# Weight splits of the even layer: three buffers for the high and low parts, two for the raw units, splits three units ahead

## The chip, the cores and the metric

The kernel runs on one core of a Trainium2 chip. The metric is the device time of one execution in microseconds (us). A difference of 0.2%, 2.4 us here, is about what its measurement can tell from no change. The core has five engines with in-order instruction queues: PE (TensorE, the matrix multiplies), DVE (VectorE), ACT (ScalarE), POOL (GpSimd) and SP (SyncE), which here issues nearly all transfers.

## The reference, cut to what matters

Two residual layers on `x` of 512 positions by 1024 channels, each followed by a squared-ReLU MLP; all in float32.

```python
def even_mixer(h, w_in, ..., w_out):
    proj = h @ w_in                       # u, q, k, v
    u = proj[..., :S5_WIDTH]
    q, k, v = jnp.split(proj[..., S5_WIDTH:], 3, axis=-1)
    q = rotary(rmsnorm(heads(q), q_g))
    k = rotary(rmsnorm(heads(k), k_g))
    y_a = s5_mixer(u, ...)                # state-space scan, gelu, gate
    y_b = dilated_attention(q, k, heads(v))
    return jnp.concatenate([y_a, y_b], axis=-1) @ w_out

for layer in range(2):
    h = rmsnorm(x, norm_mix_g[layer])
    x = x + (even_mixer(h, ...) if layer == 0 else mlstm_mixer(h, ...))
    h = rmsnorm(x, norm_mlp_g[layer])
    x = x + jnp.square(jax.nn.relu(h @ w1)) @ w2
```

## The kernel before, in words

**Weights.** Every weight matrix comes in units of 128x1024 floats. A unit is loaded into a raw buffer `wr` (L147), ACT copies it to a rounded high part `wh` (L160), and DVE subtracts to get the low part `wl` (L161). A product is then three multiplies: high by high, high by low, low by high (`mm3`, L172), so one unit of a projection is 24 multiplies of 128x512. `w_init` gets the list of units in the order in which they are used. `w_next` (L165) hands out the next unit, and `w_pump` (L151), called before and after, issues transfers and splits for the units that follow. In the even layer (`wp2` is None) there are three raw buffers and two pairs of `wh` and `wl`; transfers are issued three units ahead and splits made two ahead. From the first MLP on, `wp2` adds a third pair, and both distances grow by one.

**The even layer.** `EVEN_SEQ` (L30) writes out the order of its steps by hand: `u0` to `u3` project the state-space inputs; `a0` to `a3` and `b0` to `b3` the two halves of q and k; `v0` to `v3` the values; `n` and `r` normalise and rotate q and k; `C`, `K`, `E`, `T`, `B`, `O` and `G` are the state-space steps for one of four groups of channels Q; `h0` to `h34` are the attention steps; `X`, `Y` and the output projection close it. Counted from 0 in the order of use, the weight units are u0 a0 b0 u1 a2 u2 v0 v1 u3 v2 v3 b2 a1 a3 b1 b3, then two units of the gate and eight of the output projection. A scheduler takes the steps in that order, lets instructions that would wait be overtaken, and fixes the order of each engine's queue when the program is built. On the chip a queue stays in that order.

**Steps that the prediction speaks of.** `s5_params` (L488) computes the state-space coefficients; part of it runs on POOL (`gt`, L543) and ends in `s_pis`, `s_la` and `s_lb`. `s5_rot` (step `E`, L600) builds a table of rotations in `x` tiles by doubling: per step DVE multiplies with `s_pr`, multiplies with `s_pis` into a temporary `w0`, adds, and ACT copies halves across (L619, L620); then ACT makes `E` from it. `powers` (L628) makes `Z` and `CG`, with its temporary `w1`. `s5_in` (step `B`, L689) multiplies with `E`, scans (L710), multiplies again and gets `W`; ACT copies halves of `psa` and `W` across into `x` tiles (L705, L713). `s5_out` (step `O`, L724) sends its result through DRAM (tiles `du`), and `s5_gelu` (L741) takes it from there. `qk_rot` (L807) makes `rA` and `rB` from a transposed factor and sends them to the q and k tiles. `att_init` (L860) takes over the buffer `hg` of the activations when the last projection has read it, and loads the mask into it (`in_amask`). `att_scores` (L870) multiplies q and k on PE, adds the mask on DVE with a running maximum (L881, result `nm`), and takes the exponential on ACT (L885, after a table load).

Of the kernel before, what the change touches and what calls it, by code (L numbers as in the profile page):

```python
# [9 lines left out]
F32 = mybir.dt.float32  # L10
F32R = mybir.dt.float32r
# [5 lines left out]
P = 128  # L17
# [44 lines left out]
class Trunk:  # L62
# [67 lines left out]
            self.nc.sync.dma_start(out=self.dbg[name], in_=ap)  # L130


    AHEAD_DMA = 3
    AHEAD_SPLIT = 2
    RAW_BUFS = 3
    MORE_DMA = 1

    def w_init(self, units):
        self.wp2 = None
# [2 lines left out]

    def w_dma(self, n):
        while self.wd < n:
            r = self.t(self.wp, (P, 1024), "wr", F32, self.RAW_BUFS)
            u = self.units[self.wd]
            self.dma(r, u() if callable(u) else u)  # L147
            self.raw[self.wd] = r
            self.wd += 1

    def w_pump(self):  # L151
        n = 0 if self.wp2 is None else 1
        self.w_dma(min(self.wi + self.AHEAD_DMA + n * self.MORE_DMA, len(self.units)))
        while self.wsx < min(self.wi + self.AHEAD_SPLIT + n, len(self.units)):
            r = self.raw.pop(self.wsx)
            third = self.wp2 is not None and self.wsx % 3 == 2
            pool, bufs = (self.wp2, 1) if third else (self.wp, 2)
            h = self.t(pool, (P, 1024), "wh", F32R, bufs)
            l = self.t(pool, (P, 1024), "wl", F32R, bufs)
            self.copy_act(h, r)  # L160
            self.sub(l, r, h.bitcast(F32))  # L161
            self.split[self.wsx] = (h, l)
            self.wsx += 1
# [436 lines left out]
    def s5_rot(self, pool, Q):  # L600
        nc = self.nc
        gs = slice(8 * Q, 8 * Q + 8)
        v3 = lambda t: t.rearrange("p (g k) -> p g k", k=64)
        A, S = v3(self.xt(6)), v3(self.xt(7))
        nc.vector.memset(A[0:64, :, 0:1], 1.0)
        nc.vector.memset(A[64:128, :, 0:1], 0.0)
        nc.vector.memset(S[0:64, :, 0:1], 0.0)
        nc.vector.memset(S[64:128, :, 0:1], 1.0)
        self.copy_act(A[:, :, 1], self.e1[:, 0, gs])
        self.copy_act(S[:, :, 1], self.e1[:, 1, gs])  # L610
        for m in range(1, 6):
            n = 1 << m
            b = lambda x: x[:, m - 1, gs].unsqueeze(2).to_broadcast([P, 8, n])
            w = self.t(pool, (P, 8, n), "w0")
            self.mul(A[:, :, n:2 * n], A[:, :, 0:n], b(self.pr))
            self.mul(w, S[:, :, 0:n], b(self.pis))
            self.add(A[:, :, n:2 * n], A[:, :, n:2 * n], w)
            if m < 5:
                self.copy_act(S[0:64, :, n:2 * n], A[64:128, :, n:2 * n])  # L619
                self.copy_act(S[64:128, :, n:2 * n], A[0:64, :, n:2 * n])  # L620
        E = self.t(pool, (P, 2, 8, 64), "E", bufs=2)
        self.copy_act(E[0:64, 0], A[0:64])
        self.copy_act(E[64:128, 0], A[0:64])
        self.act(E[0:64, 1], A[64:128], AF.Copy, scale=-1.0)
        self.copy_act(E[64:128, 1], A[64:128])
        self.s5e[Q] = E
# [772 lines left out]
```

## Time and profile before

| | us |
|---|---|
| median of 3 runs | 1186.29 (1185.99 to 1187.22) |
| the profiled execution, whole | 1185.93 |
| its span, first to last instruction | 1184.1 |
| PE busy in it | 1161.5 (98%) |
| DVE busy | 813.4 (69%) |
| ACT busy | 643.1 (54%) |
| POOL busy | 64.1 (5%) |

Times inside the trace run from the start of the span. The even layer's projections stand in the first 134 us, its attention from there to about 208 us, its output projection to about 222 us; MLP, odd layer and second MLP follow. "Idle before" an instruction is the time in which its engine stood still, with the instruction that ended it. The granted clock is that of TensorE, 1.00 for 2.4 GHz and 0.50 for 1.2 GHz; a stretch in between is a mixture of the two.

### The profile page before, as it was taken

To read this page: it belongs to the slowest core of one execution; us is meant where nothing else is said; L and a number is where in the kernel's file an instruction comes from. 1 tells how busy PE (TensorE), PEld (TensorE's weight loads), DVE (VectorE), ACT (ScalarE), POOL (GpSimd) and SP (SyncE) were. 2 spreads that over 40 slices of the span, in tenths; PEclk is the share of its full clock that TensorE was granted. 3 is DMA by queue.
4 is the path that set the end of the run, shared out by engine and by line. 5 is a ranking of instruction groups with operands and counts; after the bars stand their busy time and mean duration, and the time that the engine had idled before them with its cause. 6 is when DMAs were issued, how large, how long until landed. Compare 5 with 4: busy or idle time off the path is not lost.

```text
span 1184.1 us, 15701 instructions
## 1 busy us (share of the span) xinstructions
PE 1161.5 (98%) x5540; PEld 956.2 (81%) x5540; DVE 813.4 (69%) x1466; ACT 643.1 (54%) x1162; POOL 64.1 (5%) x121
## 2 busy tenths in 40 slices
PE   6989999999999999999999999999999999999998
PEld 5868776788888888888888888887888888888887
DVE  8799864666457447779858975865664574477796
ACT  5467777444434446666656645544444444456664
POOL 0522220000000000000100000000000000000000
PEclk9989999999999999999999999999999999999999
DMA  6434531359999335565624333222599994346654
GB/s 236 125 95 122 143 79 58 121 202 370 351 345 357 122 120 160 194 195 172 188 90 153 107 108 107 81 89 72 182 353 367 345 350 144 111 157 195 208 185 158
DMA packets 73869, 216.56 MB, mean 183 GB/s; under 512 B 16888, under 2 KB 17992, under 8 KB 73792
## 3 DMA queue, kind: packets, MB, share of 16 engines
q1 hardware_dynamic: 72576, 214.27, 53.7%
q0 software_dynamic: 1216, 1.31, 0.5%
q8 instruction: 43, 0.70, 0.2%
q14 instruction: 34, 0.28, 0.1%
HBM read 175.14 MB, written 38.31 MB: 180 GB/s over the span
## 4 chain that ended last, share of the span: by engine, by line
PE 92%; DVE 3%; ACT 1%; POOL 1%; issue 1%; DMA 1%; SPq 0%; DVEq 0%; ACTq 0%
PE acc L123 79%; PE psa L123 8%; PE psb L123 3%; DVE wl L96 1%; PE psb L898 1%; POOL rA L543 1%; PE psb L281 1%; ACT wh L120 0%; ACT hg L117 0%; DVE hg L108 0%; DMA hg<-in_amask 0%; DMA wr<-in_w_l 0%; DVE x L108 0%; PE psb L1207 0%; DVE x L96 0%
## 5 line engine op out<-in xcount | busy, mean ns | idle before, releaser
L123 PE MATMUL acc<-hg,wh 128*128 128x512 f32 x1600 | 500.7, 393 | 8.8 <-ACT hg L117 7.2
L120 ACT ACTIVATE wh<-wr 128x1024 fp32r<-128x1024 f32 x243 | 257.2, 1060 | 398.1 <-PE acc L123 321.3
L96 DVE TENSOR_TENSOR wl<-wr,wh 128x1024 fp32r<-128x1024 f32 x243 | 297.3, 1224 | 221.5 <-ACT wh L120 211.4
L123 PEld LDWEIGHTS acc<-hg,wh 128*128 128x128 f32 x1600 | 298.7, 188 | 70.1 <-ACT hg L117 7.2
L123 PE MATMUL acc<-hg,wl 128*128 128x512 f32 x800 | 313.6, 392 | 0.6 <-DVE wl L96 0.6
L123 PE MATMUL acc<-wh,sp 128*128 128x512 f32 x768 | 223.0, 389 | 0.0
L123 PEld LDWEIGHTS acc<-hg,wl 128*128 128x128 f32 x800 | 150.7, 188 | 31.9 <-DVE wl L96 1.1
L123 PEld LDWEIGHTS acc<-wh,sp 128*128 128x128 f32 x768 | 144.2, 188 | 30.0
L123 PE MATMUL acc<-wl,sp 128*128 128x512 f32 x384 | 135.9, 390 | 0.8 <-DVE wl L96 0.8
L120 ACT ACTIVATE sp<-s 128x256 fp32r<-128x256 f32 x224 | 89.8, 409 | 6.8 <-PE acc L123 5.7
L96 DVE TENSOR_TENSOR tq<-tq,tq 128x1024 f32<-128x1024 f32 x64 | 78.2, 1222 | 21.0 <-DMA tq<-in_w2s 20.0
L96 DVE TENSOR_TENSOR sp<-s,sp 128x256 fp32r<-128x256 f32 x224 | 86.8, 417 | 1.4 <-ACT sp L120 1.4
L123 PEld LDWEIGHTS acc<-wl,sp 128*128 128x128 f32 x384 | 71.9, 188 | 16.6 <-DVE wl L96 1.6
L123 PE MATMUL acc<-wh,hg 128*128 128x512 f32 x192 | 63.0, 402 | 5.4 <-ACT wh L120 5.4
L123 PEld LDWEIGHTS acc<-wh,hg 128*128 128x128 f32 x192 | 36.6, 193 | 13.2 <-ACT wh L120 5.8
L123 PE MATMUL psa<-wh,sp 128*128 128x512 f32 x128 | 42.0, 389 | 0.0
L117 ACT ACTIVATE rr<-acc 128x512 f32<-128x512 f32 x72 | 41.6, 578 | 0.0
L117 ACT ACTIVATE s<-rr 128x512 f32<-128x512 f32 x64 | 40.4, 631 | 1.0
L123 PE MATMUL acc<-wl,hg 128*128 128x512 f32 x96 | 38.5, 401 | 0.3 <-DVE wl L96 0.3
L108 DVE SCALAR_TENSOR_TENSOR sf<-zb,cvw,sf 128x512 f32<-128x512 f32 x48 | 35.3, 747 | 2.3 <-ACT sf L117 1.8
L96 DVE TENSOR_TENSOR x<-x,acc 128x512 f32<-128x512 f32 x16 | 10.8, 686 | 29.3 <-PE acc L123 29.2
L123 PE MATMUL acc<-y,wh 128*128 128x512 f32 x96 | 30.0, 394 | 0.0
(324 smaller groups left out, 1327.7 us busy)
## 6 DMA issues: line engine op xcount, KB each, us to landing
wr<-in_w_l SPq DMA_DIRECT2D x67, 512.0 KB, 3.5
wr<-in_w SPq DMA_DIRECT2D x64, 512.0 KB, 5.2
tq<-in_w2s SPq DMA_DIRECT2D x64, 512.0 KB, 6.3
T<-tq SPq DMA_DIRECT2D x64, 512.0 KB, 4.8
wr<-T SPq DMA_DIRECT2D x64, 512.0 KB, 3.3
wr<-in_w2s SPq DMA_DIRECT2D x48, 512.0 KB, 4.0
x<-in_xT SPq DMA_DIRECT2D x16, 256.0 KB, 4.1
na<-scr SPq DMA_DIRECT2D x8, 256.0 KB, 3.7
```

Of the source, the lines that this page charges most:

```text
L96: return self.nc.vector.tensor_tensor(out=o, in0=x, in1=y, op=op)
L108: return self.nc.vector.scalar_tensor_tensor(out=o, in0=x, scalar=s, in1=y, op0=op0, op1=op1)
L117: return self.nc.scalar.activation(o, x, f, bias=bias, scale=scale, **kw)
L120: return self.nc.scalar.activation(o, x, AF.Copy)
L123: return self.nc.tensor.matmul(o, l, r, start=start, stop=stop)
L281: self.nc.tensor.transpose(p[:, k * P:(k + 1) * P], self.x[4 * n + k][:, t * P:(t + 1) * P], self.ident)
L543: gt = lambda o, x, y, op: self.nc.gpsimd.tensor_tensor(out=o, in0=x, in1=y, op=op)
L898: self.nc.tensor.transpose(t[:, k * P:(k + 1) * P], p[:, k * P:(k + 1) * P], self.ident)
```

## The change

In the even layer there are now three pairs of `wh` and `wl` and two raw buffers. Splits are made three units ahead and transfers issued four ahead. From the first MLP on the third raw buffer comes from `wp2`, and transfers go five ahead; there are three pairs and three raw buffers there as before. The temporary `w0` of `s5_rot` no longer has a tile of its own: it uses the tile `x2`, which `s5_in` uses too.

```diff
-    AHEAD_DMA = 3
-    AHEAD_SPLIT = 2
-    RAW_BUFS = 3
-    MORE_DMA = 1
+    AHEAD_DMA = 4
+    AHEAD_SPLIT = 3
...
     def w_dma(self, n):
         while self.wd < n:
-            r = self.t(self.wp, (P, 1024), "wr", F32, self.RAW_BUFS)
+            second = self.wp2 is not None and self.wd % 3 == 2
+            r = self.t(self.wp2 if second else self.wp, (P, 1024), "wr", F32, 1 if second else 2)
...
     def w_pump(self):
         n = 0 if self.wp2 is None else 1
-        self.w_dma(min(self.wi + self.AHEAD_DMA + n * self.MORE_DMA, len(self.units)))
-        while self.wsx < min(self.wi + self.AHEAD_SPLIT + n, len(self.units)):
+        self.w_dma(min(self.wi + self.AHEAD_DMA + n, len(self.units)))
+        while self.wsx < min(self.wi + self.AHEAD_SPLIT, len(self.units)):
             r = self.raw.pop(self.wsx)
-            third = self.wp2 is not None and self.wsx % 3 == 2
-            pool, bufs = (self.wp2, 1) if third else (self.wp, 2)
-            h = self.t(pool, (P, 1024), "wh", F32R, bufs)
-            l = self.t(pool, (P, 1024), "wl", F32R, bufs)
+            h = self.t(self.wp, (P, 1024), "wh", F32R, 3)
+            l = self.t(self.wp, (P, 1024), "wl", F32R, 3)
...
-            w = self.t(pool, (P, 8, n), "w0")
+            w = self.xt(2)[:, 0:8 * n].rearrange("p (g k) -> p g k", k=n)
```

The number of instructions on each engine stays as it was. What changes is the order in the queues: on PE, DVE and ACT in the even layer alone, on SP in the MLPs too. In the rows below the last number of a name counts tiles in the order in which the program made them, so it differs between the two kernels.

The first place is DVE's queue around the subtraction for unit 9 (v2), `wl_811` before and `wl_787` now. `x_86` before and `x_89` now is the table of step `E0`; `CG` belongs to step `K`; `wl_781` is the subtraction for unit 8. Before:

```order
L96 TENSOR_TENSOR wl_781<-wr_697,wh_780 128x1024
L96 TENSOR_TENSOR w_134_741<-x_133_734,s_pis_273 128x16
L96 TENSOR_TENSOR w_83_476<-bin_414,s_lb_317 128x8x48
L605 MEMSET x_132_733 64x8
L606 MEMSET x_132_733 64x8
L96 TENSOR_TENSOR CG_474<-CG_474,w_83_476 128x8x48
L96 TENSOR_TENSOR x_132_733<-x_132_733,s_pr_272 128x8x2
L96 TENSOR_TENSOR w_84_480<-bin_414,s_lb_317 128x8x48
L96 TENSOR_TENSOR x_132_733<-x_132_733,w_134_741 128x8x2
L96 TENSOR_TENSOR CG_474<-CG_474,w_84_480 128x8x48
L96 TENSOR_TENSOR x_132_733<-x_132_733,s_pr_272 128x8x4
L96 TENSOR_TENSOR wl_811<-wr_778,wh_810 128x1024
```

Now:

```order
L96 TENSOR_TENSOR x_94_520<-x_90_495,s_pis_273 128x128
L96 TENSOR_TENSOR x_89_494<-x_89_494,x_94_520 128x8x16
L96 TENSOR_TENSOR x_89_494<-x_89_494,s_pr_272 128x8x32
L96 TENSOR_TENSOR wl_787<-wr_703,wh_786 128x1024
L96 TENSOR_TENSOR x_95_526<-x_90_495,s_pis_273 128x256
L96 TENSOR_TENSOR x_89_494<-x_89_494,x_95_526 128x8x32
L604 MEMSET x_136_740 64x8
L605 MEMSET x_136_740 64x8
L96 TENSOR_TENSOR CG_480<-bin_420,s_la_316 128x8x48 x3
L96 TENSOR_TENSOR CG_845<-bin_677,s_la_316 128x8x48 x2
L96 TENSOR_TENSOR x_137_747<-x_136_740,s_pis_273 128x16
```

The subtraction for unit 9 has moved from behind most of step `K` to the middle of step `E0`. The one for unit 8 stands still earlier, ahead of the instruction that writes `s_pis`, as the one for unit 7 does. Ahead of POOL's part of `s5_params`, whose first instruction waits for a DVE instruction on `sf`, stand the subtraction for unit 6 and the two `x<-acc,r` of u0 and u1, which before stood behind it.

The second place is DVE's queue at the first mask sum of the attention (`nm_1550` before, `nm_1556` now). Before:

```order
L96 TENSOR_TENSOR CG_1495<-CG_1495,w_296_1505 128x8x48
L96 TENSOR_TENSOR wi_1453<-wi_1453,x_283_1454 128x512
L96 TENSOR_TENSOR wl_1513<-wr_1408,wh_1512 128x1024
L710 SCALAR_TENSOR_TENSOR W_1460<-ss_1441,wi_1453 128x512
L108 SCALAR_TENSOR_TENSOR qkv_1563<-vc_385,psb_1554 128x16
L108 SCALAR_TENSOR_TENSOR qkv_1587<-vc_385,psb_1578 128x16
L881 ISA hg_1543,nm_1550<-psa_1547,hg_1543 128x128
L881 ISA nm_1550 128x1
L96 TENSOR_TENSOR wi_1462<-W_1460,E_1368 128x512
```

Now:

```order
L96 TENSOR_TENSOR CG_1501<-CG_1501,w_299_1511 128x8x48
L96 TENSOR_TENSOR y_346_1708<-x_294_1498,y_346_1708 128x512
L96 TENSOR_TENSOR wi_1459<-wi_1459,x_286_1460 128x512
L108 SCALAR_TENSOR_TENSOR qkv_1569<-vc_391,psb_1560 128x16
L707 SCALAR_TENSOR_TENSOR W_1466<-ss_1447,wi_1459 128x512
L96 TENSOR_TENSOR wi_1468<-W_1466,E_1374 128x512
L96 TENSOR_TENSOR x_289_1469<-x_289_1469,E_1374 128x512
L717 MEMSET W_1474 128x8
L108 SCALAR_TENSOR_TENSOR qkv_1593<-vc_391,psb_1584 128x16
L878 ISA hg_1549,nm_1556<-psa_1553,hg_1549 128x128
L878 ISA nm_1556 128x1
```

Everything that stood ahead of the first mask sum still does. New ahead of it are `wi_1468` and `x_289` of step `B3`, the low part `y` of the gelu of step `G1`, and further up the subtraction for unit 18 (the first of the output projection). The instructions of step `E3`, which stood apart with those of steps `r0` and `r2` between them, now follow one another without a break, behind the subtraction for unit 17.

## Rows read from the trace of the kernel before

**Rows 1.** The page: busy us and share of the span of each engine.
```profile
PE 1161.5 (98%) x5540; PEld 956.2 (81%) x5540; DVE 813.4 (69%) x1466; ACT 643.1 (54%) x1162; POOL 64.1 (5%) x121
```
**Rows 2.** PE's waits: who waited for whom, us in total, times, longest.
```profile
PE acc L123 <- ACT wh L120: 5.8, 3, 5.4
```
**Rows 3.** Busy by stretch: start:end, us, PE PEld DVE ACT POOL, PEclk, DMA.
```profile
67.90:134.00 66.10, 66.09 (x404) 57.28 (x405) 64.19 (x149) 46.51 (x90) 12.03 (x17) 0.98 0.45 129
134.00:146.00 12.00, 11.54 (x75) 7.83 (x74) 9.69 (x27) 11.81 (x26) 6.13 (x2) 0.86 0.44 131
146.00:208.00 62.00, 60.58 (x357) 42.94 (x357) 35.76 (x93) 46.34 (x109) 8.66 (x16) 1.00 0.25 68
222.00:1185.00 963.00, 956.29 (x4415) 794.84 (x4413) 638.33 (x1004) 495.34 (x849) 14.72 (x36) 1.00 0.58 197
```
**Rows 4.** PE in order of time: start us, us, instruction [idle before <-releaser].
```profile
65.57 2.07 PE L123 MATMUL acc<-wh,hg 128*128 128x512 f32 x4 [5.39 <-ACT wh L120]
67.91 0.79 PE L123 MATMUL acc<-wl,hg 128*128 128x512 f32 x1 [0.27 <-DVE wl L96]
137.56 4.38 PE L123 MATMUL psa<-k,hg 128*128 128x128 f32 x8
```
**Rows 5.** Busy by stretch, behind PE's long wait.
```profile
65.57:70.20 4.63, 4.36 (x9) 2.97 (x10) 4.63 (x14) 1.03 (x5) 0.00 (x0) 0.50 0.55 176
70.20:75.00 4.80, 4.80 (x38) 3.70 (x36) 3.99 (x13) 2.04 (x6) 0.00 (x0) 0.99 0.10 42
```
**Rows 6.** ACT in order of time, around the long wait of PE.
```profile
61.27 1.27 ACT L120 ACTIVATE E<-x 64x512 f32<-64x512 f32 x2 [1.16 <-DVE x L96]
64.47 1.04 ACT L120 ACTIVATE wh<-wr 128x1024 fp32r<-128x1024 f32 x1
```
**Rows 7.** Busy by stretch, before the attention.
```profile
17.60:62.00 44.40, 42.54 (x206) 35.48 (x206) 37.50 (x130) 18.86 (x51) 19.42 (x42) 1.00 0.41 119
62.00:138.20 76.20, 72.36 (x444) 62.46 (x444) 74.00 (x168) 54.49 (x105) 13.24 (x20) 0.96 0.45 130
```
**Rows 8.** The chain that ended last, at the attention's start: start us, us, what.
```profile
134.26 3.82 DMA hg<-in_amask
138.23 0.29 DVE hg L881
...
139.83 1.28 ACT L117
```
**Rows 9.** DVE in order of time.
```profile
46.58 1.11 DVE L96 TENSOR_TENSOR x<-acc,r 128x512 f32<-128x512 f32 x1 [2.69 <-PE acc L123]
48.51 0.30 DVE L112 TENSOR_SCALAR s_pis<-s_pis,cst 128x160 f32<-128x160 f32 x1 [0.81 <-POOL s_pis L543]
...
125.53 1.19 DVE L96 TENSOR_TENSOR wl<-wr,wh 128x1024 fp32r<-128x1024 f32 x1
126.65 0.68 DVE L96 TENSOR_TENSOR rA<-ev,sf 128x512 f32<-128x512 f32 x1
127.25 0.68 DVE L96 TENSOR_TENSOR rB<-ev,sf 128x512 f32<-128x512 f32 x1
```
**Rows 10.** POOL in order of time, in its part of `s5_params`.
```profile
38.15 0.43 POOL L543 TENSOR_TENSOR rA<-rA 128x32 f32<-128x32 f32 x2 [35.53 <-DVE sf L96]
...
42.89 1.10 POOL L543 TENSOR_TENSOR s_pis<-rA 128x32 f32<-128x32 f32 x1
...
45.25 0.24 POOL L543 TENSOR_TENSOR s_pis<-rA 128x32 f32<-128x32 f32 x1
```
**Rows 11.** ACT in order of time, copies across of steps `E` and `B`, then the first exponential.
```profile
106.29 0.47 ACT L120 ACTIVATE x<-x 64x32 f32<-64x32 f32 x2 [0.90 <-DVE x L96]
...
138.54 1.27 ACT L120 ACTIVATE x<-W 64x512 f32<-64x512 f32 x2
...
141.12 0.40 ACT L117 ACTIVATE hg<-hg,nm 128x128 f32<-128x128 f32 x1
```
**Rows 12.** The page's DMA issues: KB each, median us from issue to landing.
```profile
na<-scr SPq DMA_DIRECT2D x8, 256.0 KB, 3.7
```

## The prediction

> **What bounds the kernel now.** I read the page first: PE is busy 1161.5 us of 1184.1 [rows 1], so all that any change could still win is 22.6 us of idle PE, and the question is where that idle time lies. The view of waits shows one large wait that concerns weights: PE waits for `wh` 5.8 us in three waits, one of them 5.4 [rows 2]. The list of PE in order of time puts it at 60 us: 5.39 us of idle before the multiply at 65.57, and 0.27 more for the `wl` of the same unit [rows 4]. It is unit 9, v2, the place that the first pair of order rows shows. Then I asked what made it late. On ACT the copy `wh` of that unit starts at 64.47, behind copies to `E` that had themselves waited for DVE's table of step `E0` [rows 6]. That table waits for `s_pis`, which POOL hands over at 48.51 [rows 9]. So the weight is late because its split stands in the queue behind a chain that has nothing to do with it. The wait has an aftermath: from 65.57 to 70.20 the granted clock is 0.50, the 1.2 GHz level, and PE gets through 9 multiplies in 4.63 us, where in the next 4.80 us at 0.99 it gets through 38 instructions [rows 5].
>
> A wait that goes on PE is only won if what follows on PE can start sooner. From 67.9 to 134 PE never stands still [rows 3]; then comes the attention, and the chain of waits says who sets its start: the mask transfer from 134.26, which waits for the last projection on PE, then DVE's first mask sum at 138.23, then ACT's table load until 141.11 [rows 8], then the first exponential at 141.12 [rows 11]. The second engine of that chain is the surprise. From 62.00 to 138.20 DVE is busy 74.00 of 76.20 us [rows 7]: it arrives at the mask sum at the same moment as the mask does. So DVE is a second bound, as tight as PE, over the whole stretch that a faster PE would want to shorten. From 146 to 208 PE is busy 60.58 of 62.00 us [rows 3], and from 222 on 956.29 of 963 us: what the first exponential gains or loses reaches the end, bar some 1.4 us of idle that the attention holds.
>
> **The change part by part.** I sum to the first exponential, against the profiled execution of 1185.93 us; the median is 0.36 us above it.
>
> *Removed: the wait for unit 9.* Its subtraction and copy stand earlier, in the middle of step `E0`; units 7 and 8 are split before `s_pis`. PE is then up to 8.0 us further: 5.39 and 0.27 of idle, and 2.3 of low clock (4.63 us at 0.50 instead of 0.99, half of it). PE alone would finish the last projection at 126, and the mask would be there at 126.3 + 3.8 = 130.1. By the next items DVE is not, so the 8.0 us turn into idle PE before the attention. I count them as zero here and in full in the rival.
>
> *Added ahead of the first mask sum on DVE.* The subtraction for unit 18, the low part `y` of the gelu, and `wi` and `x` of step `B3` now stand ahead of it. From start to start a subtraction takes 1.12 us and an operation of 128x512 takes 0.60 [rows 9]: 1.12 + 3 x 0.60 = 2.9 us. They left the attention, where DVE has time (35.76 busy of 62.00 [rows 3]), so they give little back there.
>
> *Moved: POOL's chain starts later.* It starts at 38.15 when DVE releases it through `sf` [rows 10]. Ahead of that release now stand a split (1.12) and two `x<-acc,r`. One such row says 1.11 from start to finish [rows 9], the same shape out of SBUF 0.60 from start to start; I take 0.7 each, 2.5 in all. And the subtraction of unit 8 now runs while POOL works. POOL operations of 128x32 show 0.24 us, and 1.10 for one while DVE did a large operation [rows 10]; so the bounds for one more split are 0 and 0.86, and I take 0.7. `s_pis` comes at 48.51 + 3.2 = 51.7. In that time DVE does the two splits that it did later before, 2.2 us, so DVE loses 0.9 to 1.0; I take 0.9. The Trainium skill (SBUF — State Buffer, section "SBUF: two separate sides") says that a DVE operation with two SBUF inputs and a GpSimd operation that reads SBUF take the same port pair under an exclusive lock, the loser standing still for the whole instruction. By that rule a split can hold POOL up for its whole length of 1.12, and `s_pis` would come at 52.1, 0.4 later in the sum. The lengthened POOL row agrees in kind, though it does not show whose instruction held it.
>
> *New waits on DVE.* The order makes four; none is in the trace, so each is bounded by rows.
> - `s5_in` multiplies with a copy that ACT makes, and ACT's queue now has the four copies to `E` of the next group ahead of it: two pairs of 1.27 [rows 6]. Between 0 and 2.5 us; I take 2.5, since DVE's queue holds nothing else to do there.
> - Step `E3` ran between other work and now runs in one piece. Each of its four doublings waits for two ACT copies: 0.47 for a pair, 0.90 with the gap that ACT itself had [rows 11]. Four times 0 to 0.9; I take 0.5 each, 2.0.
> - The gelu's `y` stands earlier and waits for a transfer through DRAM, on SP behind those of q and k. The nearest row, a transfer of 256 KB, takes 3.7 us from issue to landing [rows 12]: 0 to 3.7; I take 1.5, less than half, since it is issued a few instructions ahead.
> - `x` of `B3` waits for a pair of copies of 1.27 [rows 11]: I take half, 0.6.
>
> *Cover.* Against this, the 2.2 us that DVE still stood idle from 62 to 138.2 [rows 7] can be used up.
>
> *The rest.* `w0` in the tile `x2` makes step `E` and step `B` share a buffer; the steps of one group already follow each other through the rotation table, so the price is inside the waits above. In the MLPs the splits keep their order and transfers are issued one earlier into as many buffers. PE stands idle 6.7 us of 963 there [rows 3], which is the most that could be won; a raw buffer that is late would block SP, with other transfers behind it, and cost as much. I take 0: PE is fed in that stretch.
>
> *The sum.* The mask sum comes at 138.2 + 2.9 + 0.9 + 2.5 + 2.0 + 1.5 + 0.6 - 2.2 = 146.4. The table is loaded by then, since ACT has nothing in front of it, so the first exponential follows the sum of 0.3 [rows 8] at about 146.8, 5.7 later than 141.12. The attention gives back about 1.0 of its 1.4 us of idle, because some DVE work has left it. The low clock at its start stays: the stretch from 134 to 146 stands at 0.86 now [rows 3], with eight score multiplies taking 4.38 us [rows 4], and it will follow the longer idle too. Net +4.7: 1190.6, and **1191.0** against the median.
>
> Bounds: with all four waits covered the mask sum comes at 139.8, the exponential is held by the table load at about 141, and the end is 0 to 1 earlier, 1185.3. With all at their upper bound it is 5.1 more, 1196.
>
> **The rivals.**
> 1. *Faster: PE's gain is kept.* DVE stood idle 6.9 of 44.40 us from 17.6 to 62 [rows 7], 2.69 of it for PE and 0.81 for POOL in two rows alone [rows 9]. If the splits that now stand there fill this time, and the four waits are covered because all inputs come earlier, DVE reaches the mask sum between 138.2 + 2.9 - 6.9 - 2.2 = 132.0 (no idle at all) and 136.5 (half of it left). The exponential comes 4 to 9 us earlier: 1177 to 1183. For it: each piece of PE work that feeds DVE comes earlier. Against it: POOL's chain is released later, not sooner. Chance 0.25.
> 2. *No difference: 1184 to 1188.7.* The gain before 62 us and the new waits cancel, or the table load keeps the exponential at 141. For it: the lower bound of my own sum. A difference under 0.2%, 2.4 us, is one that a measurement can't tell from none. Chance 0.20.
> 3. *Slower still: the gelu's transfer waits on SP behind a weight transfer.* With transfers four ahead and two raw buffers, SP waits for a raw buffer until DVE has made a split, and DVE waits for the gelu's transfer behind it. It decides if the wait passes its upper bound of 3.7 us; then the end is above 1193, up to 1197. Against it: the splits concerned stand ahead on DVE. Chance 0.10, within the 0.55 of slower.
>
> That the change does not do what it says is excluded by the order: every split stands one unit earlier.
>
> **How the numbers follow.** My forecast's case, slower, has 0.55 with rival 3; faster by over 0.2% has 0.25, the rest 0.20. The range reaches down to 1181, where half of rival 1 lies outside, and up to 1196.5, the upper bound of the waits: about 0.2 is left out. The likeliest case's own range is 1188.7 to 1196.
>
> **What would show it.** Right: no PE wait at 60 us and no low clock behind it; PE idle before the attention by 10 us or more; `s_pis` near 51.7; DVE waiting for ACT in steps `E3` and `B`; the first exponential near 147. Wrong: a first mask sum before 138, DVE with less idle before 138 than the 9.1 us of now, which would mean that the new waits are covered; or a shift of PE's time behind 222 us, which would mean that the MLPs' transfers count.

## The result, and the profile after

| | before | after |
|---|---|---|
| median, us | 1186.76 (4 runs) | 1198.99 (4 runs, 1198.29 to 1200.39) |
| ratio to before | | 1.0105, 95% interval 1.0088 to 1.0123 |
| span of the profiled execution, us | 1184.1 | 1196.8 |
| first mask sum (DVE), first exponential (ACT) | 138.2, 141.1 | 150.6, 151.2 |

The change makes the kernel 12 us slower. The prediction said slower, by 4.2, with a range up to 1196.5: the side is right, the size is not. Two kernels further down, `E3_first` and `weights_O1late`, had one execution each in a slower state of the chip (1970.7 and 6706.6 us), which their medians count and their ratios leave out.

First the busy line of the page after, which answers to [rows 1]:

```profile
PE 1165.6 (97%) x5540; PEld 959.3 (80%) x5540; DVE 815.6 (68%) x1466; ACT 644.7 (54%) x1162; POOL 66.3 (6%) x121
```

The same 5540 multiplies take PE 4.1 us longer than before, and span less busy time, PE's idle time, went from 22.6 to 31.2 us. 4.1 and 8.6 make the 12.7 us by which the span grew. So there are two losses to find: idle time, and slower multiplying.

PE in order of time, after: its waits over 1 us from 55 us to the attention. The last two columns say how long PE stood idle ahead of the instruction, and for whom:

```profile
61.40 0.50 PE L123 MATMUL acc<-wl,hg 128*128 128x512 f32 x1 [1.49 <-DVE wl L96]
69.53 0.50 PE L123 MATMUL acc<-wl,hg 128*128 128x512 f32 x1 [1.27 <-DVE wl L96]
75.45 1.06 PE L646 MATMUL psb<-cst,Z 128*128 128x128 f32 x8 [1.05 <-DVE Z L96]
85.99 0.74 PE L123 MATMUL acc<-hg,wh 128*128 128x512 f32 x2 [1.46 <-DVE x L96]
123.46 1.06 PE L646 MATMUL psb<-cst,Z 128*128 128x128 f32 x8 [2.88 <-DVE Z L96]
142.01 0.59 PE L123 MATMUL psb<-cst,ev 128*128 128x4 f32 x2 [6.72 <-ACT ev L117]
```

The wait for unit 9 [rows 4] is gone, and its place is taken by smaller ones of the same sum: the first four and one of 0.16 make 5.4 us. Then come two that were not there, 2.88 and 6.72. The last of them stands ahead of step `n3`. The projections end at 129.1 instead of 134.2, but that is no lead: step `O1`, 5.3 us of PE, stood ahead of the last of them before and stands behind it now. The multiplies ahead of `n3` are the same 640 in both kernels, and PE is through them 1.2 us later than before, with 16.4 us of idle time on the way instead of 14.6. Busy by stretch (columns as in [rows 3]), before and after:

```profile
0.00:134.06 134.06, 119.50 (x640) 100.01 (x641) 121.46 (x333) 82.85 (x169) 34.61 (x67) 0.97 0.48 147
0.00:135.32 135.32, 118.94 (x640) 98.77 (x640) 117.57 (x318) 81.22 (x165) 36.22 (x67) 1.00 0.45 141
```

Busy by stretch, after: from the start to the first mask sum; the stretch around it; from a point in the first MLP, with the same 4279 multiplies left to do in both kernels, to the end.

```profile
0.00:150.63 150.63, 127.42 (x676) 106.52 (x676) 131.27 (x344) 90.43 (x180) 39.27 (x68) 0.95 0.45 141
136.00:156.00 20.00, 13.50 (x60) 10.18 (x61) 15.85 (x36) 13.28 (x26) 6.70 (x2) 0.50 0.37 105
264.80:1196.80 932.00, 925.95 (x4279) 769.41 (x4277) 617.95 (x979) 482.62 (x831) 14.71 (x36) 1.00 0.58 200
```

And the two rows of the kernel before that answer to the first and the last:

```profile
0.00:138.23 138.23, 123.67 (x676) 104.00 (x676) 125.40 (x340) 86.96 (x176) 34.78 (x68) 0.98 0.49 149
252.80:1184.10 931.30, 925.49 (x4279) 769.32 (x4278) 619.88 (x980) 483.49 (x832) 14.72 (x36) 1.00 0.58 200
```

From that point on both kernels take the same time, 932.0 and 931.3: the earlier transfers in the MLPs are worth nothing that can be measured. Ahead of the first mask sum DVE has 131.27 us of work in 344 instructions instead of 125.40 in 340, and stands idle 19.4 us instead of 12.8. Behind PE's 6.72 us of idle time the granted clock is 0.50, 1.2 GHz, for the whole stretch from 136 to 156.

ACT in order of time, after, at the end of that wait:

```profile
138.78 1.27 ACT L120 ACTIVATE E<-x 64x512 f32<-64x512 f32 x2 [2.26 <-DVE x L96]
...
141.36 0.60 ACT L117 ACTIVATE ev<-acc 128x512 f32<-128x512 f32 x1
...
149.91 1.28 ACT L117 ACT_TABLE_LOAD   x1
151.21 0.40 ACT L117 ACTIVATE hg<-hg,nm 128x128 f32<-128x128 f32 x1
```

`ev<-acc` is the square of a sum that PE had finished some 27 us earlier (step `a3`, unit 13). It stands behind the copies to `E3`, and these wait for DVE, where the last doubling of `E3` starts at 132.66 and ends at 138.74 with the first operations of `r2` and the subtraction for unit 18 in between: only the first four doublings follow one another without a break. Before, the square ran at 127.5. The chain that ended last, after, from there to the first mask sum:

```profile
141.36 0.61 ACT ev L117
141.97 0.04 issue
142.01 6.99 PE psb L123 x32
149.00 1.50 PE psa L123 x4
150.50 0.06 issue
150.56 0.09 DVE qkv L108
150.64 0.05 DVE hg L878
```

The 32 multiplies are those of `n3` and `n1`. At 0.50 they take 7.0 us; before they took 3.5 (134.07 to 137.56 [rows 4]). DVE's own queue reaches the mask sum at the same moment, so the trace does not tell which of the two set it.

At the other end of DVE's queue, POOL and DVE in the part of `s5_params`, after:

```profile
40.82 0.82 POOL L540 TENSOR_TENSOR rA<-rA 128x32 f32<-128x32 f32 x2 [38.19 <-DVE sf L96]
47.18 1.34 POOL L540 TENSOR_TENSOR rA<-s_pis 128x32 f32<-128x32 f32 x1
```

```profile
47.19 1.22 DVE L96 TENSOR_TENSOR wl<-wr,wh 128x1024 fp32r<-128x1024 f32 x1
52.52 0.30 DVE L112 TENSOR_SCALAR s_pis<-s_pis,cst 128x160 f32<-128x160 f32 x1 [4.10 <-POOL s_pis L540]
```

POOL's chain starts 2.7 us later than before [rows 10] and ends at 52.5. The POOL operation that runs beside the subtraction of unit 8 takes 1.34 us where 0.24 is usual.

### The profile page after: what moved, and what is told of

It reads as the page before. It is cut to its first block, busy times and chain, and to the rows that moved or that the text cites. A ratio compares the mean times of both kernels' runs of the same rounds, so it can differ in the third digit from the quotient of the medians.

```text
span 1196.8 us, 15704 instructions
## 1 busy us (share of the span) xinstructions
PE 1165.6 (97%) x5540; PEld 959.3 (80%) x5540; DVE 815.6 (68%) x1466; ACT 644.7 (54%) x1162; POOL 66.3 (6%) x121
## 4 chain that ended last, share of the span: by engine, by line
PE 87%; DVE 7%; ACT 2%; issue 2%; POOL 1%; DMA 1%; SPq 0%; DVEq 0%; ACTq 0%
PE acc L123 74%; PE psa L123 7%; PE psb L123 3%; DVE wl L96 2%; DVE x L96 1%; PE psb L895 1%; POOL rA L540 1%; PE psb L278 1%; ACT x L120 1%; DVE CG L96 0%; DVE sf L108 0%; ACT hg L117 0%; DVE w L96 0%; ACT wh L120 0%; DMA bin<-in_s_bc 0%
## 5 line engine op out<-in xcount | busy, mean ns | idle before, releaser
L96 DVE TENSOR_TENSOR x<-x,acc 128x512 f32<-128x512 f32 x16 | 10.8, 687 | 28.4 <-PE acc L123 28.3
```

The costliest lines, as they stand in the source:

```text
L96: return self.nc.vector.tensor_tensor(out=o, in0=x, in1=y, op=op)
```

## The experiments

All 18 experiments in one table, under the two kernels. "Idle" is span less PE's busy time, from the page; "PE busy" shows the clock, since the multiplies are the same (2.9 us of useless multiplies are in it where "+12" stands, 9.4 where "+27"); "clock" is the granted clock of the stretch from 130 to 170 us; "first exp." is the start of the first exponential. The last four columns are of one execution, the profiled one, which is not always near the median: that of before_less_DVE took 1189.45 us, that of weights_only, 1200.04, was the slowest of its five.

| kernel | median, us | ratio to before, 95% interval | idle | PE busy | clock | first exp. |
|---|---|---|---|---|---|---|
| before | 1186.76 | | 22.6 | 1161.5 | 0.96 | 141.1 |
| after | 1198.99 | 1.0105 (1.0088 to 1.0123) | 31.2 | 1165.6 | 0.74 | 151.2 |
| share_only | 1202.18 | 1.0137 (1.0118 to 1.0156) | 29.7 | 1169.3 | 0.74 | 146.0 |
| weights_only | 1199.22 | 1.0096 (1.0082 to 1.0109) | 28.3 | 1169.7 | 0.70 | 151.5 |
| E3_first | 1205.32 | 1.0153 (1.0139 to 1.0167) | | | | |
| weights_warm (+12) | 1193.70 | 1.0056 (1.0042 to 1.0069) | 23.9 | 1167.6 | 0.83 | 147.3 |
| weights_O1late | 1204.21 | 1.0141 (1.0126 to 1.0157) | 30.3 | 1171.3 | 0.62 | 146.1 |
| weights_both (+12) | 1204.41 | 1.0145 (1.0131 to 1.0159) | 28.7 | 1173.8 | 0.66 | 147.8 |
| after_warm (+27) | 1199.06 | 1.0102 (1.0088 to 1.0116) | 24.1 | 1174.0 | 0.91 | 151.7 |
| after_inplace | 1197.30 | 1.0090 (1.0077 to 1.0103) | 28.7 | 1166.7 | 0.79 | 150.7 |
| weights_inplace_warm (+12) | 1195.82 | 1.0077 (1.0064 to 1.0089) | 26.3 | 1168.0 | 0.83 | 148.4 |
| before_inplace | 1186.86 | 1.0001 (0.9992 to 1.0010) | 22.8 | 1162.5 | 0.96 | 141.9 |
| after_both | 1197.38 | 1.0088 (1.0074 to 1.0102) | 28.7 | 1166.8 | 0.87 | 146.4 |
| after_r2first | 1202.92 | 1.0143 (1.0127 to 1.0159) | 31.7 | 1168.9 | 0.70 | 139.7 |
| before_both | 1188.97 | 1.0015 (1.0007 to 1.0024) | 24.5 | 1161.8 | 1.00 | 140.8 |
| after_C3 | 1197.16 | 1.0095 (1.0081 to 1.0110) | 29.9 | 1165.3 | 0.79 | 141.5 |
| after_n2 | 1200.39 | 1.0114 (1.0100 to 1.0129) | 32.9 | 1166.2 | 0.83 | 147.3 |
| before_C3 | 1189.51 | 1.0031 (1.0019 to 1.0042) | 25.0 | 1163.3 | 0.91 | 142.6 |
| after_less_DVE | 1196.46 | 1.0081 (1.0068 to 1.0094) | 31.5 | 1164.5 | 0.83 | 148.9 |
| before_less_DVE | 1191.97 | 1.0047 (1.0033 to 1.0061) | 24.7 | 1163.0 | 0.91 | 142.2 |

Of E3_first only the time is used.

**Which part of the change.** With the result known, the shared tile `x2` looked guilty: with it, the doublings of step `E3` stand behind step `B2`. Two kernels take the change apart, a third turns the order of the tile's users round.

share_only, the kernel before with:

```diff
-            w = self.t(pool, (P, 8, n), "w0")
+            w = self.xt(2)[:, 0:8 * n].rearrange("p (g k) -> p g k", k=n)
```

> The kernel before with one part of the change alone: the temporary w0 of the rotation table lies in the tile x2. Buffers and distances of the weights stay as before. Theory A (the shared tile is the main cost): step E3 can't write its temporary before step B2 has read x2 for the last time, so DVE's queue holds E3 in one piece behind B2, ACT's copies to E3 come late, and the ACT copies that empty the sums of the last projection stand behind them; the first mask sum comes 6 to 10 us later than 138.2, the time is 1192 to 1197 us. Theory B (the step of the prediction: splits moved ahead, POOL's later chain and new waits that come with the splits): the tile is free of cost, 1185 to 1188 us.

weights_only, the changed kernel with:

```diff
-            w = self.xt(2)[:, 0:8 * n].rearrange("p (g k) -> p g k", k=n)
+            w = self.xt(1)[:, 0:8 * n].rearrange("p (g k) -> p g k", k=n)
```

> The changed kernel, with the temporary w0 in the tile x1, which nothing needs between the loads of x and step O1, in place of x2: the whole change of weight buffers and distances, without the sharing between steps E and B. Theory A: E3 runs between other work again, PE keeps a part of the 5.4 us that it waited at 60 us, the first mask sum comes at 133 to 139, the time is 1180 to 1187 us. Theory B: the splits cost the same without the shared tile, first mask sum at 144 to 148, the time is 1189 to 1195 us.

E3_first, the changed kernel with:

```diff
-C3 B2 r2 E3 a3 b1 B3
+E3 C3 B2 r2 a3 b1 B3
```

> The changed kernel, where the hand-written order has E3 ahead of C3, B2 and r2 in place of behind them: the tile x2 is still shared, but E3 takes it first and B2 has to wait. Theory A: the order of the two users of x2 decides; E3 is early, the last projection's sums are emptied in time, but step B2 is late by some us; 1184 to 1193 us. Theory B: no difference from the changed kernel beyond 2 us, 1197 to 1201 us.

Measured: 1202.2, 1199.2 and 1205.3. Each half of the change costs 12 to 15 us alone, both together 12. Theory A falls with weights_only, theory B with share_only; each also misses the size in the kernel that speaks for it, and E3_first lies above both ranges. weights_only is not free of sharing: `x1` is the tile that `O1` writes, so `E3` is now tied to `O1`. The new buffers with `w0` in a tile of its own were not tried. What the first two have in common with the changed kernel is in the last columns of the table: 6 to 9 us more idle time, 4 to 8 us more busy time at a clock of 0.70 to 0.74.

In share_only the attention starts at 146.0 and then stalls: from the first exponential to the end it takes 1053.0 us, the kernel before 1043.0 and the changed one 1045.6. Work that was done ahead of the attention now stands directly ahead of it and inside it. ACT in order of time:

```profile
142.15 1.27 ACT L120 ACTIVATE E<-x 64x512 f32<-64x512 f32 x2 [1.87 <-DVE x L96]
...
144.73 1.28 ACT L117 ACT_TABLE_LOAD   x1
146.03 0.40 ACT L117 ACTIVATE hg<-hg,nm 128x128 f32<-128x128 f32 x1
```

The copies to `E3` stand directly ahead of the first exponential; before they ran at 118.3.

**The clock.** weights_warm fills one wait of weights_only with multiplies into a sum that nobody reads; weights_O1late moves step `O1`; weights_both does both; after_warm fills the wait of the changed kernel.

```diff
+    def warm(self, n):
+        z = self.acc()
+        for j in range(n):
+            self.mm(z, self.hl[0][:, 0:P], self.hg[0][0], j == 0, j == n - 1)
...
-B3 O1 K3 b3 "
+B3 O1 K3 b3 Z12 "
```

> The kernel weights_only with 12 multiplies of 128x512 added behind the last projection, of the last weight unit with the first activations into a sum that nobody reads: 2.8 us of work that lies where PE stood idle 2.50 us (126.3 to 128.8). All else keeps its order. Theory C (the clock): the wait there lets the granted clock fall to 0.50 for 24 us, and PE's work up to the attention and in its first steps, 22 us of busy time in that stretch, takes twice as long; with the gap filled the clock stays at 1.00 for steps O1 and n3, the first exponential comes at 140 to 146 in place of 151.5, the time is 1186 to 1193 us. Theory D (the queues: ACT empties the sum of the last projection only behind step O1's copy, which waits for PE): the clock is an effect and not a cause, the added work costs nothing or 1 to 3 us, 1197 to 1202 us.

```diff
-B3 O1 K3 b3 h0 n3 h1
+B3 K3 b3 h0 n3 O1 h1
```

> The kernel weights_only with step O1 moved in the hand-written order from ahead of K3 and b3 to behind n3; no multiplies added. ACT then empties the last projection's sum without waiting for O1's 32 multiplies, and PE does n3 ahead of O1. Theory D: the first exponential comes 6 to 9 us earlier, the time is 1188 to 1193 us, although the clock still falls. Theory C: O1 and n3 run at half clock in either order and the work is the same; 1194 to 1200 us.

> Both edits of weights_warm and weights_O1late together. If both matter, this is the fastest of the three: theories C and D each give 1180 to 1188 us here, the lead of PE from the wait at 60 us is kept in part. If the attention's start is held by DVE's work alone (the prediction's step), it is not below 1189 us.

after_warm, the changed kernel with 13 multiplies of the first kind and 7 on the table of `E3`:

```diff
+            self.mm(z, self.EA[:, 0:P], self.EA, j == 0, j == n - 1)
...
-B3 O1 K3 b3 "
+B3 O1 K3 b3 Z13 z7 "
```

> The changed kernel itself with PE's idle time before step n3 (135.3 to 142.0) filled by multiplies into sums that nobody reads: 13 of 128x512 with the last weight unit and 7 float32 ones that read the finished table of step E3, so that they end at about 142. No other engine gets work. Theory C: the clock stays at 1.00, n3's 32 small multiplies take 3.5 us in place of 7.0, the first exponential comes at 146 to 148 in place of 151.2, and the first scores run at full clock; 1191 to 1195 us. Theory D: no change, 1198 to 1201 us.

The first pair is the clearest experiment of the study. PE in order of time, weights_only (its two waits ahead of the attention):

```profile
128.81 1.16 PE L123 MATMUL psb<-cst,rr 128*128 128x128 f32 x8 [2.50 <-ACT BT L120]
142.43 0.59 PE L123 MATMUL psb<-cst,ev 128*128 128x4 f32 x2 [2.53 <-ACT ev L117]
```

The same place in weights_warm:

```profile
126.32 2.89 PE L123 MATMUL acc<-hg,wh 128*128 128x512 f32 x12
129.04 1.14 PE L123 MATMUL psb<-cst,rr 128*128 128x128 f32 x8
130.01 1.90 PE L123 MATMUL psa<-U,BT 128*128 128x64 f32 x16
138.01 0.59 PE L123 MATMUL psb<-cst,ev 128*128 128x4 f32 x2 [2.53 <-ACT ev L117]
```

And the stretch from 126 to 154 us of each, weights_only first:

```profile
126.00:154.00 28.00, 22.97 (x100) 20.17 (x99) 19.39 (x40) 15.25 (x28) 5.89 (x2) 0.57 0.36 110
```

```profile
126.00:154.00 28.00, 25.34 (x146) 20.43 (x144) 21.83 (x50) 19.19 (x40) 6.29 (x2) 0.76 0.40 117
```

More work, done sooner: 12 useless multiplies make the kernel 5.5 us faster, and the intervals of the two ratios lie apart. Where PE stood idle 2.50 us the clock was 0.50 from about 130 on, and `O1` and `n3` ran at half speed; where it multiplied, `O1` ran at 1.00 and `n3` started 4.4 us earlier. Up to there the two queues differ by nothing else; behind it the scheduler has also put DVE's `y` of the gelu (0.69 us) from ahead of the first mask sum to behind it, so not all of the 5.5 is the clock's. That speaks for theory C and against D, though 1193.7 us and a first exponential at 147.3 lie just outside C's ranges: the clock still falls later, around the second wait of 2.53 us.

The other three do not repeat it. weights_O1late is a miss for both theories (`n3` starts 5 us earlier, the first exponential too, and the attention then stalls, 1055.4 us from there to the end). weights_both adds nothing to it: the first wait is filled and the clock stays up there, but PE then waits 5.94 us for `n3` and stands at 0.50 behind that. after_warm, 1199.1 us, is in theory D's range and no clean test:

```profile
138.52 2.79 PE L123 MATMUL acc<-hg,wh 128*128 128x512 f32 x11
141.16 6.17 PE L123 MATMUL acc<-x 128*128 128x512 f32 x14
```

The seven float32 multiplies run as 14 and take 6.17 us, and `n3` started 5.2 us later than without them, at 147.2. About 3 of the 5.2 are not the dose: the projections themselves ended at 132.1 instead of 129.1. Both kernels have the same wait ahead of that, 2.88 us in the changed one, 2.94 here. Behind it the clock stayed at 1.00 in the one and was at 0.50 until about 129.6 in the other, first the changed kernel:

```profile
123.50:129.00 5.50, 5.50 (x29) 4.69 (x30) 5.50 (x10) 4.19 (x8) 0.00 (x0) 1.00 0.62 154
123.50:129.00 5.50, 5.43 (x17) 4.69 (x18) 5.50 (x10) 4.29 (x8) 0.00 (x0) 0.50 0.62 141
```

From `n3` to the first exponential it took 4.5 us instead of 9.2, in part because the clock was up (0.81 from 147 to 152), in part because the other engines had had more time. What the clock at 135 is worth in the changed kernel, this run does not show.

Nor does the clock need a wait of PE to fall. In the kernel before PE never stands still from 67.9 to 137.6 and ends with the 32 multiplies of 128x4; the clock is down right behind them:

```profile
134.00:137.60 3.60, 3.60 (x35) 3.56 (x33) 3.60 (x5) 3.51 (x6) 0.00 (x0) 1.00 0.72 178
137.60:141.00 3.40, 3.28 (x9) 1.58 (x9) 2.97 (x12) 3.31 (x5) 2.94 (x2) 0.65 0.66 235
```

So light multiplies are a rival of the wait: in weights_only the wait is followed by `O1`'s multiplies of 128x64, and no run varied the one without the other.

**One step behind it?** a3's square waits for one of three buffers `ev`, which the rotation `r2` on DVE gives back. after_inplace takes that wait away, weights_inplace_warm and before_inplace are its partners.

```diff
-        t1 = self.tmp("ev", bufs=3)
-        t2 = self.tmp("sf")
-        self.stt(t1, B, gB, cc, ALU.mult, ALU.mult)
-        self.stt(t2, A, gA, cs, ALU.mult, ALU.mult)
-        self.add(rB, t1, t2)
+        self.stt(cc, B, gB, cc, ALU.mult, ALU.mult)
+        self.stt(cs, A, gA, cs, ALU.mult, ALU.mult)
+        self.add(rB, cc, cs)
```

> The changed kernel, where the second pair of products of the rotation (steps r) is written over the two factors in qv and qs in place of taking one more tile ev and one more sf. Same arithmetic. The three buffers of ev are then not all held when step a3 wants one for the square of its sum: in the changed kernel that square stands on ACT at 141.4, behind the rotation r2 (138.7) and the copies to E3, though its sum was long complete. Theory E (the buffer ev ties the attention's start to r2): the square of a3 comes before the copies to E3, step n3 starts at 135 to 139 in place of 142.0, PE's idle time before it shrinks from 6.7 us to under 3, the first exponential comes at 143 to 147; 1188 to 1194 us. Theory F (DVE's work alone holds the first mask sum): n3 may start earlier, the mask sum stays at 149 to 151; 1196 to 1200 us.

> The kernel weights_warm (all of the change but the shared tile, with 12 idle multiplies) with the rotation in place as in after_inplace. ACT empties the sums of b3 and a3 one after the other ahead of the copies for B3 and O1. Theory E: n3 starts at about 135.5, when O1's multiplies end, in place of 138.0, PE waits for nothing there and the clock stays up; the first exponential comes at 141 to 145, the time is 1183 to 1190 us. Theory F: as weights_warm, 1192 to 1195 us.

> The kernel before with the rotation in place alone. There the square of a3 already follows the rotation r2 without delay (127.5), 7 us before the last projection ends. Theories E and F: no difference, 1185 to 1188 us. If it is slower, the edit itself costs, and the two kernels above have to be read with that.

The square comes early now, at 133.2 instead of 141.4, and 1197.3 is not apart from 1199.0 by the intervals: theory E, 1188 to 1194, falls. weights_inplace_warm is no faster than weights_warm, and before_inplace is as expected. The next wait took the place; ACT in weights_inplace_warm, ahead of the first exponential:

```profile
144.02 0.63 ACT L117 ACTIVATE x<-x 128x512 f32<-128x512 f32 x1 [5.77 <-DMA x<-du]
```

Here it is the gelu, behind `O1`'s way through DRAM.

**Moves in the order.** after_both and after_r2first move `r2` (and `O1`) ahead; after_C3 moves `C3`; after_n2 brings all of q and k ahead; before_both and before_C3 are the same moves in the kernel before. From a common stretch of the written order:

```diff
-B0 B1 v3 O0 K2 T1 b2 n2 a1 r0 C3 B2 r2 E3 a3 b1 B3 O1 K3 b3
+B0 B1 v3 O0 K2 T1 b2 n2 a1 r0 r2 O1 C3 B2 E3 a3 b1 B3 K3 b3
...
+B0 B1 v3 O0 K2 T1 b2 n2 a1 r0 r2 C3 B2 E3 a3 b1 B3 O1 K3 b3
...
+B0 B1 v3 O0 C3 K2 T1 b2 n2 a1 r0 B2 r2 E3 a3 b1 B3 O1 K3 b3
...
+B0 v3 O0 b2 n2 C3 B1 K2 T1 a1 r0 r2 B2 E3 a3 b1 O1 B3 K3 b3
```

> The changed kernel with two steps moved in the hand-written order: r2 and O1 stand ahead of C3, B2 and E3 in place of behind them. PE then does O1 between the projections and n3 directly behind the last one, as in the kernel before; ACT empties a3's sum before the last projection ends. Theory G (one cause: in the changed order r2 and O1 stand behind other DVE work, and what was hidden beside the projections is exposed behind them): the first exponential comes at 134 to 143 in place of 151.2, the low clock shrinks from 20 us to under 10, 1178 to 1188 us. The prediction's step (the amount of DVE work ahead of the first mask sum): the mask sum stays at 145 or later, 1191 to 1199 us.

> The changed kernel with r2 alone moved ahead of C3 and B2; O1 stays behind the last projection on PE. Theory G: a3's sum is emptied 10 us earlier and n3 no longer waits for it, but O1 still stands ahead of n3 on PE; half of the loss comes back, 1187 to 1194 us. The prediction's step: 1195 to 1200 us.

> The kernel before with the same two moves as after_both. Theory G: r2 and O1 were in time there, so little can be won, 1183 to 1189 us. If it is faster than that, the two moves are worth something of their own, and after_both has to be read against this kernel.

> The changed kernel with step C3 moved ahead of K2 in the hand-written order (before: behind r0). Theory H (C3's late transposes hold the two psb buffers that r2 and O1 need): C3's Z is done by 108, O1's multiplies lie between the projections, a3's sum is emptied before the last projection ends; the first exponential at 134 to 143, 1177 to 1188 us. If DVE's amount of work holds the start (the prediction's step): mask sum at 145 or later, 1191 to 1199 us.

> The changed kernel with b2 and n2 moved ahead of C3, B1 and K2, C3 ahead of B1, and r2 behind r0: the normalisation and rotation of q and k come first on DVE, the state-space steps behind. Theory H: as after_C3 or better, 1177 to 1188 us, since POOL's power (3.2 us) for n2 is then waited for beside other work. The prediction's step: 1191 to 1199 us.

> The kernel before with the move of after_C3. Theory H: C3 was in time there; 1183 to 1190 us. It is the kernel against which after_C3 has to be read.

Theories G and H fall: 1197.2 to 1202.9. after_r2first and after_C3 start the attention in time, the other two 5 to 6 us late, and all four lose time behind the start: 1049.1 to 1060.9 us from the first exponential to the end, against 1045.6 in the changed kernel. The prediction's step, a mask sum at 145 or later, fails in after_C3 (141.1), and after_r2first (1202.9 us) lies above the 1195 to 1200 that it gave. PE in after_C3, its first scores, and ACT in after_r2first behind its first exponential:

```profile
140.34 0.77 PE L123 MATMUL psa<-k,hg 128*128 128x128 f32 x2 [7.92 <-DMA k<-rB]
```

```profile
139.70 0.40 ACT L117 ACTIVATE hg<-hg,nm 128x128 f32<-128x128 f32 x1 [0.28 <-DVE nm L878]
...
146.14 1.28 ACT L117 ACT_TABLE_LOAD   x1 [2.04 <-DMA x<-du]
...
149.29 1.28 ACT L117 ACT_TABLE_LOAD   x1
150.58 0.51 ACT L117 ACTIVATE hg<-hg,nm 128x256 f32<-128x256 f32 x1
```

In the first, PE waits 7.92 us for a rotated k that comes from DVE by a transfer. In the second, the second exponential comes 10.9 us behind the first, because a gelu with its two table loads lies between. The two moves in the kernel before cost 0.15% and 0.31% as well, with intervals that exclude zero.

**The amount of DVE work.** Both kernels with nine DVE operations less; what they leave out is group 2's coefficients `CG`, and with them its share of the result:

```diff
-        self.powers(pool, Q, CG, B[:, 2], B[:, 3], self.la, self.lb, (0, 3, 6, 9))
+        if Q == 2:
+            self.nc.gpsimd.memset(CG, 0.0)
+        else:
+            self.powers(pool, Q, CG, B[:, 2], B[:, 3], self.la, self.lb, (0, 3, 6, 9))
```

> The changed kernel without the coefficients CG of group 2: step K2's nine DVE operations of 128x384 (0.47 us each from start to start, 4.2 us) are left out, and POOL sets CG to zero in their place; what the group gives to the result is left out with them. DVE bound (the prediction's step, with the clock on top): the first mask sum comes 4 to 7 us earlier than 150.6, and the time falls by 4 to 9 us, 1190 to 1195 us. If the clock or ACT's queue alone held the start: by less than 2 us, 1197 to 1200 us.

> The kernel before without the same nine operations of step K2, CG of group 2 set to zero by POOL. There the mask sum waits for the mask, which waits for the last projection on PE (134.2), so DVE's relief helps little: 0 to 2 us, 1184.5 to 1187 us. If it gains as much as the changed kernel does, DVE bound both kernels alike, and the change did not make DVE the bound.

The changed kernel gains 2.5 us of the 4.2, less than expected and with intervals that overlap, and its first mask sum comes 2.1 us earlier where 4 to 7 were expected: inconclusive. The kernel before becomes 5 us slower with less work, its interval clear of zero. So less DVE work alone does not buy time; in the changed kernel its share stays open. PE's largest wait in after_less_DVE is again at the sums of the projection:

```profile
143.66 0.59 PE L123 MATMUL psb<-cst,rr 128*128 128x4 f32 x2 [4.55 <-ACT rr L117]
```

**What is shown and what stays open.** Shown, in one pair: behind a wait of PE of 2.50 us ahead of the attention stood half clock; with the wait filled by useless work the next step ran at full clock, and the kernel was faster. Not shown: that this holds for each such wait (2.88 and 2.94 us had different clocks behind them), or how much of the changed kernel's 12 us it makes. Shown: taking away any one of the late steps tried (the shared tile, `ev`, `O1`, `r2`, `C3`, `n2`) does not bring the time back. Open: the amount of DVE work. Argued, not shown: the attention's start is a join of four in-order queues (the projections on PE, squares and copies on ACT, rotation and tables on DVE, the power on POOL) in an order that was fixed when the program was built, and in the kernel before it fits with 1.4 us of idle PE from 130 to 170; four of the five edits tried on that kernel made it slower, whatever they add or remove. before_inplace alone left it as it was. Why the program's scheduler orders worse after any of these edits was not tried. No version of the study beats the kernel before.

## Why the prediction was right in direction and wrong in size

- **The wait at 60 us.** Right that it goes and that no low clock follows it there (1.00 from 55 to 120). Wrong that it leaves PE free: 5.66 us became 5.4 us in five waits until 86 us. DVE is as late as it was, and PE now waits for it directly.
- **PE's lead.** "PE is then up to 8.0 us further" did not happen: it is through the 640 multiplies ahead of `n3` 1.2 us later than before, since a wait of 2.88 us came on top. The 6.72 us that PE then stands idle, less than the 10 us that the text named, are no lead turned into idle time but a new wait, and its place was not foreseen: not the mask, but a3's square on ACT. The sum counted the lead as nothing, so this did not move the number.
- **POOL's chain.** 52.5 against 51.7, with the start 2.7 us later as against 2.5. The rule in the section of the Trainium skill that was cited (SBUF — State Buffer, "SBUF: two separate sides") gave 52.1 with a split's 1.12 us from rows. The trace agrees with it better than with the 0.7 of the sum, since the POOL operation beside the split took 1.34 us, about 1.1 more than alone, the whole length of a split.
- **DVE's added work.** Forecast 2.9, measured 5.9 (131.27 less 125.40). The four added instructions are about 3.4 of it; 1.6 of the other 2.5 are in steps `E`, whose short operations follow one another and overlap less.
- **DVE's waits.** Forecast +5.3 net (0.9 + 2.5 + 2.0 + 1.5 + 0.6 - 2.2), measured +6.5 (19.4 less 12.8). One by one: the doublings of `E3` waited 0.8 us, not 2.0, the gelu's `y` 0.9, not 1.5, `x` of `B3` 0.6 as forecast; the wait for `s_pis` was 4.1 us long, where 0.8 stood before. Mask sum 150.6 against 146.4, first exponential 151.2 against 146.8. The table load was not quite out of the way: it ended at 151.19, some 0.3 us behind the sum. The upper bounds of the text add up to 4.6, not 5.1; the result lies beyond either.
- **The low clock: the step that failed.** "The low clock at its start stays", and it was priced at nothing, with 1.0 us given back by the attention. The runs showed a stretch of 20 us at 0.50 where the kernel before had only part of 12 us [rows 3]: PE's busy time grew by 4.1, although 2.3 went at 60 us; `n3` and `n1` took 7.0 us instead of 3.5; and from the first exponential to the end it took 2.6 us more instead of 1.0 less, all of it slower multiplying, first before, then after:

```profile
141.12:1184.10 1042.98, 1035.04 (x4861) 851.04 (x4860) 685.35 (x1119) 553.35 (x983) 26.46 (x53) 1.00 0.55 187
151.21:1196.80 1045.59, 1037.97 (x4864) 852.59 (x4864) 683.74 (x1120) 553.67 (x982) 26.43 (x54) 1.00 0.55 187
```

  I had the price in [rows 5], 2.3 us lost behind a wait of 5.4, and took it off at 60 us without asking what a longer idle time at 135 would cost.
- **The sum.** Forecast +4.7; DVE's work +3.0, its waits +1.2 and the part behind the first exponential +3.6 more than forecast, and 0.2 of rounding, make +12.7. So the clock is the largest single miss, 3.6 of 8.0 us, and DVE's work, sized at half of what it was, the next. The two are not independent ahead of the mask sum, where the slow `n3` and DVE's queue end together.
- **Rivals.** The faster one fell where the text said that it would, at POOL's later start: DVE's idle time from 17.6 to 62 was 7.5 us instead of 6.9, not filled. The gelu's transfer behind a weight transfer was not seen; its `y` waited 0.9 us, under the 3.7 that would have decided. Missing was a rival in which the tile shared by `E` and `B` counts: the text put its price "inside the waits above", and share_only measured 15 us for it alone.

## What to carry to other kernels

A wait removed on the busiest engine is worth only what the engines that feed the next join can follow; look there first, and price the idle time that appears in its place twice, as time and as the clock that may fall behind it. A scratch tile borrowed from another step is an edge in the graph: price it like a wait, not like memory. Where an order fixed at build time joins four queues with almost no slack, read a small edit's effect from the whole order, and expect most edits to cost.

## What the runs showed of the hardware that was not expected

Twelve multiplies whose result nobody reads, 2.89 us of PE, made a kernel 5.5 us faster (1199.2 to 1193.7), with the granted clock at 1.00 through the step behind them. A wait of 2.9 us at the same place left the clock at 1.00 in one kernel and was followed by 0.50 in another, and in the kernel before it fell behind 32 multiplies of 128x4 without any wait. And a POOL operation of 128x32 beside a DVE subtraction of 128x1024 stood 1.34 us where 0.24 is usual, about as long as the subtraction (1.22).
